# A planner that knows of the interface VectorE and GpSimd share: what a new instruction order does to a two-block kernel

## The chip, the cores and the metric

The kernel runs on one core of a Trainium2 chip. A core has engines that run their own instruction queues beside each other: TensorE (PE in the profile; PEld is its weight load), VectorE (DVE), ScalarE (ACT), GpSimd (POOL) and SyncE (SP, which issues the transfers here). The metric is the device time of one execution in microseconds, the median of several runs. Smaller is better.

## The reference

Two transformer-like blocks on 512 tokens of width 1024, all in float32:

```
first_block:  h = x + hybrid_mixer(rmsnorm(x))       # gMLP gating, a gated 31-tap convolution, an mLSTM
              h = h + cross_attention(rmsnorm(h), rmsnorm(mem))
              h = h + conv_glu(rmsnorm(h))           # width 2816
              x = rmsnorm(h)
second_block: x = layer_norm(a*x + nsa_pool_mixer(x))   # sparse attention and a pooling branch
              x = layer_norm(a*x + square(relu(x @ w1)) @ w2)    # width 4096
              x = layer_norm(a*x + gla_mixer(x))        # gated linear attention
              x = layer_norm(a*x + square(relu(x @ w1)) @ w2)
```

Nearly all of the arithmetic is in products with weights that come from HBM once.

## The kernel before

**Products in two parts.** Every float32 matrix is split into a high part, rounded to the type float32r that TensorE multiplies at its full rate, and a low part, the difference. A product is then three matmuls: high by high, high by low, low by high (`mm`). So every weight that arrives has to be split on the chip first. Weights come in units of 512 KB (`wunit`): a transfer into a raw tile `wr`, then for each half of 512 columns a cast into `wh` and a subtraction `wr - wh` into `wl`. The cast may be done by ScalarE or VectorE, the subtraction by VectorE or GpSimd. `xth`/`xtl`, `hid`, `o`, `yh`/`yl`, `v`, `ph`/`pl` are split activations, `ps` are the eight banks of PSUM in which products build up, `x` is the running state, `nat` a norm before it is transposed, `g` a norm's gain, `ident` the identity with which TensorE transposes. In the mixer `gs`, `mrun` and `mrs` hold the mLSTM's gates and their running sums (4 partitions of 512), `pw` weights made from them, and `gcv`, `tm` the sums and products of the 31-tap convolution: the products `tm` go to VectorE or ScalarE, all sums `gcv` to GpSimd.

**What sets the order.** No instruction order is written by hand. The code of the stages is run against a `Recorder`, which keeps every step with the engines that may do it. A `Plan` then plays the program with a price for each step (`price1`: microseconds on the engine) and a time after it until others see the result. At every turn each engine takes, of its ready steps that can start first, the one with the longest remaining way to the end; a step with two possible engines goes to the one on which it ends first. The plan is played again up to eight times with the latest starts of the last plan as ranks (`ROUNDS = 8`), and the shortest is kept. The kernel is then emitted in the order of the planned starts, each engine's queue in that order; only the order and the choice of engine come from the plan, the waits on the chip are semaphores. Room is planned too: 33 pages for weights and split blocks, 3 raw tiles, 8 banks. Where the plan leaves TensorE without work for over 1 us (`IDLE`) ahead of a bank's first product, `emit` fills the gap with products that nothing reads, one for each 0.216 us (`warm`: `ps<-ident`, 128x512), to keep the array's clock up. They are put into the program whether or not the gap is there on the chip.

The parts that the change touches, before it:

```
def split(...):            # of weights
    nc.add([[("scalar", "activation", (hi, src, AF.Copy), {})], [("vector", "tensor_copy", (hi, src), {})]],
           BIAS)
    self.either("tensor_sub", lo, src, hi.bitcast(F32), bias=BIAS)     # VectorE or GpSimd

def price1(eng, m, args, kw):    # for TensorE
    return max(n, 2 * width(args[1])) / 2400.0 + 0.0025

def run(self, prio=None):        # the choice of engine for a step with two forms
    if any(max(ready[i], free[x[0]]) + x[2] + x[4] < mine - 1e-9 for x in o.forms if x[0] != e):
        continue
```

`BIAS` (1.0 us) is added to VectorE's end when it is compared with the other engine's for a weight's cast or subtraction: VectorE gets the step only where it would end over 1 us earlier. The plan's own prices, which the change leaves, put a subtraction of 128x512 at half as much on VectorE as on GpSimd. In the trace all instructions carry line 487, the line of `emit` that issues them; in the changed kernel it is 509.

Of the kernel before, what the change touches and what calls it, by code (L numbers as in the profile page):

```python
# [14 lines left out]
PSUM = bass.MemoryType.PSUM  # L15
# [13 lines left out]
# room: pages of weights or of a split block, half pages, weights on their way in  # L29
# [5 lines left out]
BIAS = 1.0  # L35


class Op:
    """One step of the plan: instructions that one engine issues back to back."""
# [20 lines left out]
def run(ap):  # L60
    """Elements next to each other in a transfer."""
    n = 1
    for s, k in sorted((int(s), int(k)) for s, k in list(ap.ap)[1:]):
        if s != n:
            break
        n *= k
    return n


def region(ap):  # L70
    """The tile, the partitions and the set of elements (as bits) that an access touches."""
# [26 lines left out]
class Recorder:  # L98
    """Stands in for the engines: keeps what they are told to do for the plan."""
# [9 lines left out]
    def add(self, forms, bias=0.0):  # L109
        """forms: ways to do one step, each a list of calls to one engine; bias: time against VectorE's."""  # L110
# [17 lines left out]
        o.forms = [(f[0][0], f) + price(f) + (bias if f[0][0] == "vector" else 0.0,) for f in forms]  # L128
# [3 lines left out]
    @contextmanager  # L132
    def together(self):
        """Calls to one engine as one step."""
        self.held = []
        yield
        calls, self.held = self.held, None
        self.add([calls])
# [11 lines left out]
def price1(eng, m, args, kw):  # L150
# [5 lines left out]
    if eng == "tensor":  # L156
        if m == "transpose":
            return 0.109
        if "float32r" in str(args[1].dtype):
            return max(n, 2 * width(args[1])) / 2400.0 + 0.0025  # L160
        return 4 * max(n, 64) / 2400.0
# [25 lines left out]

def price(calls):
    """Time on the engine, and the time after it until others see the result."""
# [5 lines left out]
class Plan:  # L195
    """Orders the recorded steps: each engine takes the ready step with the longest way to the end."""
# [16 lines left out]
    def depend(self):  # L213
# [29 lines left out]
        # weights wait for an earlier unit's end, and nothing starts too far ahead of its use  # L243
# [17 lines left out]
        # late banks are taken when all that goes into them is there  # L261
# [30 lines left out]
    def rank(self):  # L292
        for o in reversed(self.ops):
            eng, _, d, lat, _ = o.forms[0]
# [12 lines left out]
    def run(self, prio=None):  # L307
        ops, N = self.ops, len(self.ops)
        P = prio or [o.prio for o in ops]
        free = dict.fromkeys(Recorder.ENGINES, 0.0)  # L310
        dma_issue = dma_data = 0.0
# [17 lines left out]
        def room(o):  # L329
            """Time from which the step's new tiles find room; None if they may not be taken yet."""  # L330
# [32 lines left out]
        for _ in range(N):  # L363
            best = None
            for e, q in queue.items():
# [4 lines left out]
                for i in q:  # L370
                    o = ops[i]
                    s = ready[i] if ready[i] > f else f
                    if mn is not None and s > mn:
                        continue
                    form = next(x for x in o.forms if x[0] == e)
                    if len(o.forms) > 1:
                        mine = s + form[2] + form[4]
                        if any(max(ready[i], free[x[0]]) + x[2] + x[4] < mine - 1e-9 for x in o.forms if x[0] != e):
                            continue
# [29 lines left out]
            _, calls, d, lat, _ = form  # L409
# [7 lines left out]
            else:  # L417
# [4 lines left out]
                end = free[e] = s + d  # L422
            o.start, o.end, o.pick, o.room = s, end, calls, taken
# [19 lines left out]
    def improve(self, n):  # L443
        """Plans again with the last plan's latest starts as ranks, and keeps the best plan."""
# [8 lines left out]
    def late(self):  # L453
        """Latest starts of the steps when each engine keeps its order, as priorities."""
# [16 lines left out]
    def emit(self, tc, warm):  # L471
        """warm: calls that keep the array's clock up, for a bank about to be used."""
# [17 lines left out]
class Split:  # L490
    """A float32 matrix as two float32r parts whose sum is exact."""
# [11 lines left out]
class Duo:  # L503
    """Two 128-row blocks of a split matrix, as one operand of the vector engines and as blocks."""
# [6 lines left out]
class Block:  # L511
# [19 lines left out]
    # ---- room  # L531
    def rules(self, quota, banks=(2, 10), pages=(2, 1000), halves=(0, 1000)):
        """For the steps from here on: units of weights at a time; of each kind of room, what a step ahead of
        its turn leaves free for those before it, and how many of them it may pass."""
# [3 lines left out]
    def ps(self, late=False):  # L538
        """A bank; late: not taken before all that goes into it is there."""
# [8 lines left out]
    def pair(self, s):  # L548
        """A split block of 512 columns in one page."""
# [19 lines left out]
    # ---- building blocks  # L569
    def warm(self, bank):  # L570
        """A product that nothing reads: TensorE runs at half its clock after some microseconds without work."""
# [10 lines left out]
    def turn(self, ps, srcs):  # L582
        """Transposes of 128-column pieces next to each other in a bank."""
# [4 lines left out]
    def either(self, method, *args, bias=0.0, **kw):  # L588
        """A step for VectorE or GpSimdE."""
# [19 lines left out]
    def wunit(self, loads, n=1024):  # L609
        """Streams one unit of weights in; loads: (view of the unit, DRAM source)."""  # L610
# [12 lines left out]
    def unit_t(self, w, c0):  # L623
        """128 columns of a [1024, n] weight."""
# [4 lines left out]
    def unit_n(self, w, r0):  # L629
        """128 rows of a [k, 1024] weight."""  # L630
        return self.wunit([(lambda r: r, w[r0:r0 + P, :])])

    def proj_t(self, u, xT):
        """One column block; the first ones of a stage go by halves of the tokens."""
# [8 lines left out]
    def rsqrt(self, v, mul, eps, v2=None):  # L643
        """(v * mul + eps) ** -0.5 by Newton's iteration from an integer seed; v2 adds to v."""
# [22 lines left out]
    # ---- norms between the stages  # L667
# [4 lines left out]
    def to_T(self, src, i):  # L672
        """Token tile i of natural activations into blocks."""
# [9 lines left out]
    def rms(self, x, g, n, fast=True):  # L683
        """n = norm of x."""
# [13 lines left out]
    def stats(self, x, n=512):  # L698
        """Mean and variance along the free axis, by pieces of n."""
# [17 lines left out]
    def rms_norm_x(self, g):  # L717
        """The norm in the place of x."""
# [45 lines left out]
    def tail(self, steps, norm, turn=True):  # L764
        """A stage's last projection and the norm after it, by token tiles."""
# [13 lines left out]
    def proj_n_steps(self, part, w, r0, alpha=None, us=None, fine=False):  # L779
        """x += part.T @ w[r0:], part: blocks; fine: smaller pieces for the last tokens."""  # L780
# [17 lines left out]
    def setup(self):  # L798
# [11 lines left out]
        # additive causal mask of a diagonal tile  # L810
# [7 lines left out]
    def pack(self, names):  # L818
        """Vectors of a multiple of 128 as columns, 128 to a column."""
# [19 lines left out]
    # ---------------------------------------------------------------- block 1  # L839
    def mix(self):  # L840
# [10 lines left out]
        # gates: the parts of their weights next to each other  # L851
# [44 lines left out]
        # xc, its convolution, and q, k, v  # L896
# [16 lines left out]
        def qkv(h):  # L913
# [10 lines left out]
            # two more columns of ones sum the rows of the scores  # L924
# [6 lines left out]
        # score rows of the key tiles: 0, 1 and 3 in a page, 2 in half of one  # L931
# [86 lines left out]
        # gated convolution  # L1018
# [11 lines left out]
        def taps():  # L1030
            """The convolution's taps: products on VectorE and ScalarE, sums on GpSimdE."""
# [38 lines left out]
        # spatial gating  # L1070
# [123 lines left out]
    def gate_proj(self, gu, xT):  # L1194
        """Both parts of narrow weights side by side in the columns, their products in the rows."""
# [10 lines left out]
    def mem(self):  # L1206
        """Keys and values of the memory."""
# [113 lines left out]
    # ---------------------------------------------------------------- block 2  # L1321
# [21 lines left out]
    def nsa(self, xT):  # L1343
# [5 lines left out]
        def stack(t, ps, g, scale=None):  # L1349
            """64 rows of group g as hi and lo halves of the 128 rows of t."""  # L1350
# [23 lines left out]
        def compress(s):  # L1374
            """Compressed keys (s = 0) or values of both groups."""
# [46 lines left out]
            else:  # L1422
                # rows: hi and lo parts of the scores, for each the blocks of both groups
# [8 lines left out]
        # keys with both halves of the rows alike: all hi, all lo  # L1432
# [12 lines left out]
        # queries: hi and lo halves of the rows, in heads b and 4 + b  # L1445
# [11 lines left out]
        # values and gates, token-major  # L1457
# [23 lines left out]
        # pooling branch  # L1481
# [32 lines left out]
        def cmp_attn(b, q):  # L1514
            """Attention of a pair of heads over the compressed blocks: gated scores, by blocks."""
# [360 lines left out]
```

## Time and profile before

| | |
|---|---|
| median of 3 runs | 2028.74 us (2028.26 to 2033.82) |
| profiled execution | span 2026.6 us from its first to its last instruction; the page gives no other time of it |
| PE | 1931.1 us busy, 95% |
| DVE | 1283.8 us busy, 63% |
| ACT | 804.4 us busy, 40% |
| POOL | 714.8 us busy, 35% |
| HBM | 177 MB moved, 88 GB/s |

Rows of groups read: line, engine, operation, out<-in with the buffers' numbers left out, sizes, how many, then busy time in us and mean ns of one, then idle time of that engine just before them and who ended it. Rows by stretch of time read: from:to, length, busy us (and instructions) of PE, PEld, DVE, ACT and POOL, the share of TensorE's clock that was granted, the share of time that DMA was busy, GB/s. In time: the first block's mixer runs to about 300 us, with the memory's keys and values from about 195; cross attention to about 450; the convolutional feed-forward to about 815; sparse attention to about 1050; the first MLP to about 1400; linear attention to about 1640; the second MLP and the last norm to the end.

### The profile page before, as it was taken

What the parts mean: (1) busy time and instruction counts of PE and PEld (TensorE: products, weight loads), DVE (VectorE), ACT (ScalarE), POOL (GpSimd) and SP (SyncE); (2) the same over time, 40 slices, a digit from 0 to 9 for tenths busy, and PEclk for the clock granted to TensorE, in tenths of its full rate; (3) what the DMA queues carried; (4) which work ended last, traced back from release to release, by engine and by line L of the source; (5) the groups of instructions that cost most, each with busy time, mean ns of one, the idle gap of its engine ahead of it and who ended that gap; (6) DMA issues with size and microseconds to landing.
All of it is one profiled execution on the core that took longest, in us unless ns stands there. A gap on an engine that the chain in (4) does not pass through costs nothing. (4 is left out here: it accounts for less than half of the span.)

```text
span 2026.6 us, 27236 instructions
## 1 busy us (share of the span) xinstructions
PE 1931.1 (95%) x10206; PEld 1632.6 (81%) x10206; DVE 1283.8 (63%) x2366; ACT 804.4 (40%) x1614; POOL 714.8 (35%) x571
## 2 busy tenths in 40 slices
PE   8978899999999999989999999999999999999998
PEld 7756778888888888878888777777999888778776
DVE  5899966564444456588984345467686774355457
ACT  4556435334322233576734223232465334122231
POOL 3767534213212333233644222233223234122232
PEclk9988999999999999999999999999999999999999
DMA  5212333223213333330332233332223322223231
GB/s 165 79 47 72 125 94 115 83 63 105 74 54 102 115 101 89 70 74 11 97 112 84 63 94 104 85 126 77 83 62 104 94 73 87 61 77 107 91 127 55
DMA packets 215470, 177.40 MB, mean 88 GB/s; under 512 B 25174, under 2 KB 194202, under 8 KB 215338
## 3 DMA queue, kind: packets, MB, share of 16 engines
q1 hardware_dynamic: 215338, 175.66, 29.6%
q8 instruction: 80, 1.31, 0.3%
q14 instruction: 52, 0.43, 0.1%
HBM read 173.54 MB, written 2.10 MB: 87 GB/s over the span
## 5 line engine op out<-in xcount | busy, mean ns | idle before, releaser
L487 POOL TENSOR_TENSOR wl<-wr,wh 128x512 fp32r<-128x512 f32 (+1 forms) x387 | 551.7, 1438 | 1093.3 <-PE ps L487 450.3
L487 PE MATMUL ps<-xth,wl 128*128 128x512 f32 (+1 forms) x1464 | 516.9, 353 | 4.9 <-DVE wl L487 4.3
L487 PE MATMUL ps<-xtl,wh 128*128 128x512 f32 (+1 forms) x1464 | 517.3, 353 | 3.8 <-DVE xtl L487 3.7
L487 PE MATMUL ps<-xth,wh 128*128 128x512 f32 (+1 forms) x1464 | 519.4, 355 | 0.1
L487 ACT ACTIVATE wh<-wr 128x512 fp32r<-128x512 f32 (+1 forms) x544 | 311.9, 622 | 462.9 <-PE ps L487 277.3
L487 PE MATMUL ps<-wh,hid 128*128 128x512 f32 (+1 forms) x1392 | 437.5, 392 | 1.4 <-ACT wh L487 1.3
L487 DVE TENSOR_TENSOR wl<-wr,wh 128x512 fp32r<-128x512 f32 x238 | 285.0, 1211 | 135.4 <-ACT wh L487 78.9
L487 PEld LDWEIGHTS ps<-xth,wl 128*128 128x128 f32 x1464 | 278.3, 190 | 47.0 <-DVE wl L487 5.8
L487 PEld LDWEIGHTS ps<-xtl,wh 128*128 128x128 f32 x1464 | 278.6, 190 | 44.6 <-DVE xtl L487 6.0
L487 PEld LDWEIGHTS ps<-xth,wh 128*128 128x128 f32 x1464 | 279.0, 191 | 40.1 <-ACT xth L487 0.5
L487 PEld LDWEIGHTS ps<-wh,hid 128*128 128x128 f32 x1392 | 261.1, 188 | 60.9 <-ACT wh L487 2.7
L487 PE MATMUL ps<-wl,hid 128*128 128x512 f32 (+1 forms) x696 | 275.0, 395 | 7.7 <-DVE wl L487 6.2
L487 DVE TENSOR_TENSOR x<-x,ps 128x512 f32<-128x512 f32 (+1 forms) x210 | 140.6, 677 | 155.7 <-PE ps L487 154.8
L487 PEld LDWEIGHTS ps<-wl,hid 128*128 128x128 f32 x696 | 131.2, 188 | 46.5 <-DVE wl L487 13.6
L487 DVE TENSOR_TENSOR r<-r 128x512 f32<-128x512 f32 x64 | 69.0, 1079 | 65.2 <-ACT r L487 64.7
L487 DVE CAST wh<-wr 128x512 fp32r<-128x512 f32 x81 | 45.8, 581 | 90.5 <-PE ps L487 83.7
L487 PE MATMUL ps<-wl,xth 128*128 128x256 f32 (+2 forms) x320 | 94.6, 296 | 1.3 <-DVE wl L487 1.0
L487 PE MATMUL ps<-wh,xth 128*128 128x256 f32 (+2 forms) x320 | 95.7, 299 | 0.0
L487 PE MATMUL ps<-wh,xtl 128*128 128x256 f32 (+2 forms) x320 | 94.3, 295 | 0.0
L487 POOL TENSOR_TENSOR gcv<-gcv,tm 128x511 f32<-128x511 f32 (+29 forms) x60 | 81.4, 1376 | 16.8 <-DVE tm L487 12.3
L487 DVE TENSOR_TENSOR hid<-r,hid 128x512 fp32r<-128x512 f32 x64 | 51.8, 810 | 43.0 <-ACT hid L487 42.4
L487 ACT ACTIVATE r<-ps 128x512 f32<-128x512 f32 x64 | 37.7, 589 | 90.6 <-PE ps L487 90.6
(355 smaller groups left out, 2718.2 us busy)
## 6 DMA issues: line engine op xcount, KB each, us to landing
wr<-in_mlp_w_dram SPq DMA_DIRECT2D x128, 512.0 KB
wr<-in_w_up_dram SPq DMA_DIRECT2D x44, 512.0 KB
wr<-in_c_w_in_dram SPq DMA_DIRECT2D x24, 512.0 KB
wr<-in_w_down_dram SPq DMA_DIRECT2D x22, 512.0 KB
wr<-in_w_in_dram SPq DMA_DIRECT2D x16, 512.0 KB
wr<-in_w_xkv_dram SPq DMA_DIRECT2D x16, 512.0 KB
wr<-in_w_out_dram SPq DMA_DIRECT2D x8, 512.0 KB
wr<-in_w_xq_dram SPq DMA_DIRECT2D x8, 512.0 KB
```

The costliest lines, as they stand in the source:

```text
L487: getattr(getattr(self.rec.nc, eng), method)(*args, **kw)
```

## The change

Three changes, all in the planner. (1) The interface to on-chip memory that VectorE and GpSimd share becomes a resource of the plan: `port` tells which steps need it (every GpSimd operation but fills and counters; of VectorE those with two inputs wider than one element in SBUF, and plain copies and `tensor_scalar` from SBUF to SBUF), and such a step starts only after the last one that held it. (2) `BIAS` becomes 0. (3) A matmul is priced by `n / 2285 + 0.007` us: 0.231 us in place of 0.216 for 512 columns, 0.119 in place of 0.109 for 256. Comments and docstrings are taken out besides, which does nothing.

```
-BIAS = 1.0
+BIAS = 0.0
...
-            return max(n, 2 * width(args[1])) / 2400.0 + 0.0025
+            return max(n / 2285.0 + 0.007, width(args[1]) / 1200.0 + 0.0025)
...
+def port(calls):
+
+    for eng, m, args, kw in calls:
+        if eng not in ("vector", "gpsimd") or m in ("memset", "iota", "dma_start"):
+            continue
+        out = kw["out"] if "out" in kw else args[0]
+        ins = [x for x in list(args[1:]) + [x for k, x in kw.items() if k not in ("out", "accum_out")] if is_ap(x)]
+        room = [x for x in ins if "PSUM" not in str(x.space) and width(x) > 1]
+        if eng == "gpsimd" or len(room) > 1:
+            return True
+        if m in ("tensor_copy", "tensor_scalar") and room and "PSUM" not in str(out.space):
+            return True
+    return False
...
+                    form = next(x for x in o.forms if x[0] == e)
+                    if form[5] and shared > s:
+                        s = shared
...
-                        if any(max(ready[i], free[x[0]]) + x[2] + x[4] < mine - 1e-9 for x in o.forms if x[0] != e):
+                        if any(max(ready[i], free[x[0]], shared if x[5] else 0.0) + x[2] + x[4] < mine - 1e-9
+                               for x in o.forms if x[0] != e):
...
                 end = free[e] = s + d
+                if locks:
+                    shared = end
```

The work of the program is the same; its order and the engines of some steps are not. Counted over the whole program: subtractions `wl` of 128x512 on VectorE 236 before and 537 now, on GpSimd 381 and 80; casts `wh` of 128x512 on ScalarE 536 and 406, on VectorE 81 and 211; ScalarE's table loads 45 and 40; products `ps<-ident` that nothing reads 38 and 131; SyncE's instructions 409 and 409.

TensorE's row in the mixer, around the transposes of the gates. Before, the transposes come between other products (`ps_102`, `ps_171`):

```order
L487 MATMUL ps_102_177<-wh_137_212,xth_15_90 128x512
L487 MATMUL ps_102_177<-wl_138_213,xth_15_90 128x512
L487 MATMUL ps_102_177<-wh_137_212,xtl_16_91 128x512
L487 MATMUL ps_84_159<-ident_74,gs_55_130 128x4 x4
L487 MATMUL ps_84_159<-ident_74,gs_56_131 128x4 x4
L487 MATMUL ps_112_187<-mrs_53_128,ident_74 128x512 x2
```

Now some 50 of the products that stood behind them stand ahead, and 34 products that nothing reads:

```order
L509 MATMUL ps_176_251<-xth_15_90,wl_175_250 128x512
L509 MATMUL ps_120_195<-qk_92_167,qk_94_169 128x256 x3
L509 MATMUL ps_84_159<-ident_74 128x512 x34
L509 MATMUL ps_84_159<-ident_74,gs_55_130 128x4 x4
L509 MATMUL ps_84_159<-ident_74,gs_56_131 128x4 x4
L509 MATMUL ps_112_187<-mrs_53_128,ident_74 128x512 x2
L509 MATMUL ps_182_257<-mrs_53_128,ident_74 128x512 x2
```

The gates' transposes are later in TensorE's row, with nothing useful right ahead of them. A second such place follows (21 products ahead of the first `ps<-v,ph`), and 9 and 13 stand ahead of two of the memory's products.

GpSimd's row in the mixer, where the memory's weights (`wl_416`, `wl_420`, `wl_425`) arrive beside the convolution's sums. Before:

```order
L487 TENSOR_TENSOR wl_416_491<-wr_414_489,wh_415_490 128x512 x2
L487 TENSOR_TENSOR wl_420_495<-wr_418_493,wh_419_494 128x512 x2
L487 TENSOR_TENSOR gcv_98_173<-gcv_98_173,tm_286_361 128x490
L487 TENSOR_TENSOR gcv_99_174<-gcv_99_174,tm_269_344 128x494
```

Now:

```order
L509 TENSOR_TENSOR gcv_99_174<-gcv_99_174,tm_269_344 128x494
L509 TENSOR_TENSOR gcv_99_174<-gcv_99_174,tm_271_346 128x493
L509 TENSOR_TENSOR gcv_98_173<-gcv_98_173,tm_286_361 128x490
L509 TENSOR_TENSOR cv_130_205<-cv_130_205,sig_242_317 128x512
L509 TENSOR_TENSOR gcv_98_173<-gcv_98_173,tm_316_391 128x489
L509 TENSOR_TENSOR wl_425_500<-wr_423_498,wh_424_499 128x512
```

The four subtractions of `wl_416` and `wl_420` have gone to VectorE, and one of the two of `wl_425`.

VectorE's row in the second MLP where pages come free for three units at once (`wl_2541`, `wl_2544`, `wl_2555`). Before, GpSimd does one half of each of these and VectorE the other:

```order
L487 SCALAR_TENSOR_TENSOR x_73<-x_73,ps_2506_2581 128x512
L487 CAST wh_2543_2618<-wr_2542_2617 128x512
L487 CAST wh_2554_2629<-wr_2553_2628 128x512
L487 TENSOR_TENSOR wl_2541_2616<-wr_2539_2614,wh_2540_2615 128x512
L487 TENSOR_TENSOR wl_2544_2619<-wr_2542_2617,wh_2543_2618 128x512
L487 TENSOR_TENSOR wl_2555_2630<-wr_2553_2628,wh_2554_2629 128x512
```

Now all six halves are VectorE's:

```order
L509 SCALAR_TENSOR_TENSOR x_73<-x_73,ps_2506_2581 128x512
L509 CAST wh_2543_2618<-wr_2542_2617 128x512
L509 TENSOR_TENSOR wl_2541_2616<-wr_2539_2614,wh_2540_2615 128x512
L509 CAST wh_2554_2629<-wr_2553_2628 128x512
L509 TENSOR_TENSOR wl_2544_2619<-wr_2542_2617,wh_2543_2618 128x512
L509 TENSOR_TENSOR wl_2555_2630<-wr_2553_2628,wh_2554_2629 128x512 x2
L509 TENSOR_TENSOR wl_2541_2616<-wr_2539_2614,wh_2540_2615 128x512
```

The first subtraction now stands behind one cast in place of two, and GpSimd does none of the six.

More of the change, by code (lines that the diff above doesn't have):

```diff
@@ L127, in add @@
             o.reads += [region(x) for x in ins if on_chip(x)]
-        o.forms = [(f[0][0], f) + price(f) + (bias if f[0][0] == "vector" else 0.0,) for f in forms]
+        o.forms = [(f[0][0], f) + price(f) + (bias if f[0][0] == "vector" else 0.0, port(f)) for f in forms]
         self.ops.append(o)
@@ L293, in rank @@
         for o in reversed(self.ops):
-            eng, _, d, lat, _ = o.forms[0]
+            d, lat = o.forms[0][2:4]
+            eng = o.forms[0][0]
             o.prio = max((self.ops[s].prio for s in o.succs), default=0.0) + d + lat
@@ L310, in run @@
         free = dict.fromkeys(Recorder.ENGINES, 0.0)
+        shared = 0.0
         dma_issue = dma_data = 0.0
@@ L372, in run @@
                     s = ready[i] if ready[i] > f else f
+                    form = next(x for x in o.forms if x[0] == e)
+                    if form[5] and shared > s:
+                        s = shared
                     if mn is not None and s > mn:
                         continue
-                    form = next(x for x in o.forms if x[0] == e)
                     if len(o.forms) > 1:
                         mine = s + form[2] + form[4]
-                        if any(max(ready[i], free[x[0]]) + x[2] + x[4] < mine - 1e-9 for x in o.forms if x[0] != e):
+                        if any(max(ready[i], free[x[0]], shared if x[5] else 0.0) + x[2] + x[4] < mine - 1e-9
+                               for x in o.forms if x[0] != e):
                             continue
@@ L408, in run @@
                     live[k].add(t)
-            _, calls, d, lat, _ = form
+            _, calls, d, lat, _, locks = form
             if e == "sync":
```

## The prediction

> **What bounds the kernel now.** The page first: TensorE.
>
> ```profile
> span 2026.6 us, 27236 instructions
> ...
> PE 1931.1 (95%) x10206; PEld 1632.6 (81%) x10206; DVE 1283.8 (63%) x2366; ACT 804.4 (40%) x1614; POOL 714.8 (35%) x571
> ```
>
> So TensorE sits idle for 2026.6 - 1931.1 = 95.5 us, and the change, which leaves its useful products alone, can win there or in the clock. The second view is busy time by stretch: length, then busy us (and count) of PE, PEld, DVE, ACT, POOL, the granted clock, the DMA share and rate.
>
> ```profile
> core 0: us, PE busy (x) PEld busy (x) DVE busy (x) ACT busy (x) POOL busy (x), PEclk, DMA share, GB/s
> 0.00:89.00 89.00, 75.96 (x449) 66.79 (x450) 59.39 (x110) 46.60 (x91) 41.05 (x43) 0.94 0.46 127
> 89.00:126.00 37.00, 29.14 (x135) 23.06 (x134) 36.08 (x71) 21.86 (x40) 27.14 (x22) 0.91 0.27 78
> 126.00:196.00 70.00, 55.39 (x272) 45.18 (x271) 67.78 (x186) 42.18 (x83) 48.29 (x50) 0.88 0.21 61
> 196.00:259.00 63.00, 54.45 (x327) 47.19 (x328) 60.97 (x178) 34.05 (x68) 34.88 (x26) 0.94 0.32 101
> ...
> 297.00:454.00 157.00, 149.49 (x899) 131.79 (x898) 97.51 (x198) 65.30 (x160) 51.34 (x37) 0.98 0.29 84
> 454.00:763.00 309.00, 308.57 (x1393) 252.57 (x1393) 142.86 (x176) 94.77 (x158) 87.33 (x61) 1.00 0.31 93
> 763.00:888.00 125.00, 116.44 (x711) 102.93 (x711) 83.23 (x176) 58.64 (x135) 40.05 (x37) 0.98 0.36 84
> 888.00:976.00 88.00, 85.01 (x560) 75.58 (x560) 76.68 (x217) 62.30 (x178) 28.45 (x39) 0.99 0.05 17
> 976.00:1330.00 354.00, 349.31 (x1687) 287.61 (x1687) 200.70 (x301) 125.19 (x240) 130.39 (x98) 1.00 0.32 92
> 1330.00:1396.00 66.00, 63.13 (x261) 49.29 (x260) 39.15 (x55) 15.01 (x27) 19.32 (x17) 0.97 0.37 122
> 1396.00:1626.00 230.00, 223.58 (x1585) 207.05 (x1584) 173.99 (x338) 114.55 (x214) 70.30 (x52) 1.00 0.29 83
> 1626.00:1816.00 190.00, 184.80 (x914) 154.10 (x913) 101.44 (x154) 58.77 (x110) 64.75 (x42) 0.98 0.27 78
> 1816.00:2027.00 211.00, 197.91 (x871) 159.33 (x869) 120.80 (x171) 53.68 (x94) 60.55 (x42) 0.98 0.29 93
> ```
>
> From 89 to 259 us, the mixer, VectorE is 97% busy (164.8 of 170) and TensorE idles 31.0 us; at a granted clock of 0.91, 0.88 and 0.94 another 3.3 + 8.4 + 3.8 = 15.5 us are lost. Elsewhere TensorE is the bound, VectorE about half busy, and idle time comes in pieces. So a third of what can be won lies where VectorE is the bound.
>
> Next, groups by shape: is VectorE's time its own?
>
> ```profile
> L487 DVE TENSOR_TENSOR wl<-wr,wh 128x512 fp32r<-128x512 f32 x236 | 283.0, 1213 | 135.4 <-ACT wh L487 78.9 <-PE ps L487 47.8 <-issue 7.6
> L487 DVE TENSOR_TENSOR x<-x,ps 128x512 f32<-128x512 f32 x206 | 139.0, 682 | 155.7 <-PE ps L487 154.8
> L487 DVE TENSOR_TENSOR r<-r 128x512 f32<-128x512 f32 x64 | 69.0, 1079 | 65.2 <-ACT r L487 64.7
> L487 DVE CAST wh<-wr 128x512 fp32r<-128x512 f32 x81 | 45.8, 581 | 90.5 <-PE ps L487 83.7 <-issue 3.7 <-DMA wr<-in_mlp_w_dram 2.9
> ```
>
> It is not. Three operations of one size: with one input in PSUM 682 ns, with both in SBUF 1079 and 1213. The excess over 682 alone is 236 x 0.531 + 64 x 0.397 = 151 us. GpSimd's side:
>
> ```profile
> L487 POOL TENSOR_TENSOR wl<-wr,wh 128x512 fp32r<-128x512 f32 x381 | 547.9, 1450 | 1087.0 <-PE ps L487 450.3 <-ACT wh L487 412.1 <-issue 118.0
> L487 POOL TENSOR_TENSOR gcv<-gcv,tm 128x511 f32<-128x511 f32 (+29 forms) x60 | 81.4, 1376 | 16.8 <-DVE tm L487 12.3
> ```
>
> The rule of the Trainium skill for this ("SBUF — State Buffer", Who interferes with whom) is that a VectorE instruction with two SBUF inputs and a GpSimd instruction that reads SBUF exclude each other for the whole instruction. The three rows agree with it. By it the excess could fall to nothing only where no GpSimd work is left.
>
> **The change, part by part.** *301 subtractions move from GpSimd to VectorE, 130 casts from ScalarE.* VectorE gains 301 x 0.68 = 205 us (a `wl` among the gate chain's rows below takes 0.67) and at most 130 x 0.58 = 75. GpSimd loses 301 x 1.450 = 436 us of 715; if the 151 us of waiting fall in proportion (they could stay, or go whole), 92 go. VectorE ends near 1284 + 205 + 75 - 92 = 1470 us, 74%: room everywhere but in the mixer. ScalarE loses about 81 us, which nobody waits for.
>
> *One place shows the price,* in the second MLP:
>
> ```profile
> 1750.00 1.86 DVE L487 CAST wh<-wr 128x512 fp32r<-128x512 f32 x2 [8.14 <-PE ps L487]
> 1751.79 4.04 DVE L487 TENSOR_TENSOR wl<-wr,wh 128x512 fp32r<-128x512 f32 x3
> ```
>
> ```profile
> 1750.28 4.40 POOL L487 TENSOR_TENSOR wl<-wr,wh 128x512 fp32r<-128x512 f32 x3 [29.84 <-PE ps L487]
> ```
>
> ```profile
> 1753.59 0.50 PE L487 MATMUL ps<-wl,hid 128*128 128x512 f32 x1 [1.77 <-DVE wl L487]
> ```
>
> Six subtractions and two casts take until 1755.8; TensorE waits 1.77 us for VectorE's first. With all on VectorE the first stands behind one cast and is done by 1750.0 + 0.58 + 0.68 = 1751.3, so that wait goes; all eight take about 2 x 0.58 + 6 x 0.68 = 5.2 us, no longer than now. For waits of this sort, outside the mixer, I take half of a stretch's idle time as won: none is one bound, all the other. What is late next there is ScalarE's half of the casts, or the transfer.
>
> *The gates' place (89 to 126).* VectorE's rows of the gate chain, then TensorE's:
>
> ```profile
> 79.94 0.67 DVE L487 SCALAR_TENSOR_TENSOR gs<-gs,gs 4x512 f32<-4x512 f32 x1
> ...
> 84.86 0.46 DVE L487 TENSOR_SCALAR tm<-yp,cols 128x507 f32<-128x507 f32 x1
> ...
> 88.40 0.67 DVE L487 TENSOR_TENSOR wl<-wr,wh 128x512 fp32r<-128x512 f32 x1
> 89.00 1.21 DVE L487 TENSOR_TENSOR_SCAN mrun<-gs 4x512 f32<-4x512 f32 x1
> ...
> 90.72 1.76 DVE L487 TENSOR_TENSOR gs<-gs,mrun 4x512 f32<-4x512 f32 x1
> ```
>
> ```profile
> 92.61 0.66 PE L487 MATMUL ps<-ident,gs 4*128 4x4 f32 x8
> ...
> 107.56 0.58 PE L487 MATMUL ps<-v,ph 128*128 128x258 f32 x1 [3.32 <-ACT ph L487]
> ```
>
> The chain runs for 12.6 us (79.94 to 92.5) beside useful products. In the new order its last part has only dead products beside it: 34, then 21 ahead of `ps<-v,ph`. At full clock one costs 25 / 110 = 0.227 us:
>
> ```profile
> 500.00:525.00 25.00, 25.00 (x110) 20.32 (x109) 14.30 (x16) 10.23 (x18) 6.50 (x5) 1.00 0.26 84
> ```
>
> So 55 x 0.227 = 12.5 us, in place of 7.9 idle and 3.3 of clock: -1 us, that is a loss. Bounds -6 (if the chain is late besides) and +5.
>
> *126 to 196.* Of GpSimd's 48.3 us these are subtractions:
>
> ```profile
> 126.00:196.00 70.00, 16.17 (x12) 0.88 0.21 61
> ```
>
> In the matching piece of the new order 3 of 12 are left, 14 of 17 sums, and 4 of 12 products `tm` on VectorE. What the two engines need one after the other falls by 9 x (1.35 - 0.68) + 3 x 1.36 + 8 x 0.46 = 13.8 us (16.17 / 12 = 1.35; 81.4 / 60 = 1.36; 0.46 by the row of `tm` above). The ceiling is idle and clock, 14.6 + 8.4 = 23. I take 14, bounds 0 and 23.
>
> *196 to 259.* GpSimd loses 14 of 15 subtractions, 14 x 1.35 = 19, VectorE gains 13 x 0.68 = 9, and 6 sums come later, 6 x 1.36 = 8: a net 2 to 5, and 22 dead products (5.0 us) fall in 8.6 us of idle time. I take 4, bounds -5 and 12.
>
> *The rest, half of the idle,* but for the start, where the first transfers set the time, and the last norm, which no product follows:
>
> ```profile
> 2000.00:2025.00 25.00, 16.90 (x97) 14.60 (x95) 22.76 (x55) 3.05 (x4) 7.08 (x6) 0.88 0.22 82
> ```
>
> That end holds 8.1 us and the 1.6 after it. 0 to 89 +2 of 13; 297 to 454 +3 of 7.5; 454 to 763 0; 763 to 976 +5 of 11.6; 976 to 1330 +2.5 of 4.7; 1330 to 1626 +4 of 9.3; 1626 to 1816 +3 of 5.2; 1816 on +2 of the 3.4 that the last norm leaves. Together +21.5.
>
> *Dead products elsewhere:* 93 more, 77 counted above; the other 16 x 0.227 = 3.6 us, hidden in the waits for `nat` and the sparse scores: I charge half, -2. *The price of a matmul* costs nothing by itself; 25 us hold 110 of 512 columns, so 0.231 fits the trace, and 0.216 let the plan think weights late. SyncE issues the same 409, some in another order; a raw tile is free as soon as its subtraction is done, sooner by the above.
>
> Sum: -1 + 14 + 4 + 21.5 - 2 = 36.5 us. Against the profiled span 2026.6 - 36.5 = 1990; the median is 2.1 above the span, so 1992 us.
>
> **The rivals.**
>
> *Nothing to measure.* TensorE is 95% busy and the idle time moves. If the mixer wins nothing and dead products stand where TensorE has work, 93 x 0.227 = 21.1 us eat the 21.5 won elsewhere: 2028. For it: they are executed whatever happens. Against: VectorE at 97% in the mixer leaves TensorE waiting somewhere.
>
> *Slower: VectorE's queue waits for weights.*
>
> ```profile
> ACT wh L487 <- DMA wr<-in_mlp_w_dram: 100.7, 37, 6.7
> ```
>
> ScalarE stands 100.7 us for transfers in the MLPs, up to 6.7 at once. With a third of the casts and most subtractions on VectorE the same waits stand in its row, ahead of `x<-x,ps`, `r` and `hid`, on which banks and the next products depend. If they reach TensorE in full: 2029 - 36 + 101 = 2093; it turns slower once about 42 of the 101 us reach it. Say 60%: 2053. Against: VectorE has 200.7 of 354 us busy there, and TensorE idles only 4.7 us now with ScalarE so held. The Trainium skill ("TensorE: Matmul & The Clock Gate", the part on the array) calls ScalarE's and VectorE's queues strict first-in first-out, which is what this rival needs; ScalarE's row above agrees.
>
> *The interface is nearly free.* With GpSimd at 40% of its work the mixer's waits could go almost whole: 31.0 + 15.5 us less 12.5 of dead products are 34, where I count 17: 1975. For it: what blocks VectorE there is mostly gone; against: the 60 sums `gcv` stay. The exclusion rule named above would bring the time there.
>
> **How the numbers follow.** Forecast 0.70, 1992 (its own range 1972 to 2015); free interface 0.12, 1975; nothing 0.11, 2028; slower 0.07, 2053. The range is 1965 to 2032, from the upper bounds of the mixer's terms to the case of nothing. About 0.3% is what a measurement here can tell from none: 2022.6 and 2034.8. Faster 0.82, same 0.11, slower 0.07.
>
> **What would show it.** POOL near 280 us, DVE near 1450; `wl` on VectorE below 0.9 us in the mean, `r<-r` below 0.85; 126 to 196 shorter by 10 us or more, its clock above 0.95; TensorE idle below 65 us. Wrong if the mean of `wl` stays above 1 us, if the mixer's end does not come earlier, if the 34 dead products are followed by a wait of the gates' transposes, or if `x<-x,ps` waits for its own row behind a transfer.

## The result and the profile after

The median went from 2029.67 us to 1976.53 us, a ratio of 0.9731 with a 95% interval of 0.9718 to 0.9745. The profiled executions take 2026.6 and 1975.0 us, so 51.6 us are to be found. First the changed kernel's page, its first two lines:

```profile
span 1975.0 us, 26969 instructions
...
PE 1924.9 (97%) x10299; PEld 1639.8 (83%) x10299; DVE 1280.3 (65%) x2791; ACT 744.8 (38%) x1501; POOL 258.7 (13%) x254
```

TensorE idles 50.1 us in place of 95.5. Not all of these 45.4 us are won: 93 more products that nothing reads, some 93 x 0.227 = 21 us, are counted as busy now. That the busy time falls by 6.2 us all the same means that the useful products take some 27 us less. VectorE runs 425 more instructions in 3.5 us less time. The groups by shape say how:

```profile
L509 DVE TENSOR_TENSOR wl<-wr,wh 128x512 fp32r<-128x512 f32 x537 | 374.4, 728 | 67.6 <-PE ps L509 50.0 <-ACT wh L509 12.7 <-issue 1.1
L509 DVE TENSOR_TENSOR x<-x,ps 128x512 f32<-128x512 f32 x206 | 139.3, 683 | 157.0 <-PE ps L509 156.6
L509 DVE TENSOR_TENSOR r<-r 128x512 f32<-128x512 f32 x64 | 44.2, 691 | 61.5 <-ACT r L509 61.2
L509 DVE CAST wh<-wr 128x512 fp32r<-128x512 f32 x211 | 88.7, 429 | 124.0 <-PE ps L509 73.7 <-DMA wr<-in_mlp_w_dram 35.1 <-DMA wr<-in_w_up_dram 7.3
```

The three operations of one size, which took 682, 1079 and 1213 ns, now take 683, 691 and 728. The one with an input in PSUM has not moved; the others have come down to it.

Then the stretches. Both traces are cut where TensorE has done the same amount of useful products: worth 62, 86, 130, 178 and 360 us at full clock (0.231 us for 512 columns, 0.119 for 256). As the order differs, they need not be the same products one by one. Of before:

```profile
0.00:89.20 89.20, 76.16 (x449) 66.95 (x450) 59.59 (x110) 46.80 (x91) 41.25 (x43) 0.94 0.46 127
89.20:126.10 36.90, 29.04 (x135) 22.95 (x134) 35.98 (x70) 21.66 (x40) 27.04 (x22) 0.91 0.27 78
126.10:196.20 70.10, 55.49 (x272) 45.32 (x271) 67.88 (x187) 42.38 (x84) 48.19 (x50) 0.88 0.21 61
196.20:258.80 62.60, 54.05 (x326) 46.83 (x326) 60.57 (x177) 33.65 (x68) 34.68 (x26) 0.95 0.32 102
258.80:453.80 195.00, 187.45 (x1059) 161.92 (x1059) 120.75 (x243) 76.98 (x183) 62.49 (x45) 0.98 0.32 92
453.80:2026.60 1572.80, 1528.95 (x7973) 1288.65 (x7971) 939.04 (x1585) 582.91 (x1152) 501.12 (x388) 0.99 0.29 86
```

And of the changed kernel:

```profile
0.00:77.50 77.50, 73.08 (x459) 64.85 (x460) 51.94 (x122) 40.58 (x82) 32.33 (x35) 1.00 0.51 139
77.50:129.30 51.80, 43.78 (x183) 35.09 (x182) 45.53 (x94) 38.26 (x68) 22.68 (x24) 0.87 0.26 75
129.30:184.30 55.00, 51.02 (x287) 43.06 (x287) 48.22 (x162) 37.65 (x75) 27.48 (x28) 0.97 0.17 49
184.30:244.70 60.40, 54.85 (x335) 48.49 (x335) 56.03 (x150) 33.84 (x68) 26.33 (x19) 0.97 0.41 128
244.70:432.50 187.80, 184.07 (x1064) 159.44 (x1063) 130.59 (x318) 71.37 (x172) 23.14 (x17) 1.00 0.31 94
432.50:1975.00 1542.50, 1518.09 (x7980) 1288.92 (x7978) 947.97 (x1949) 523.11 (x1040) 126.71 (x132) 1.00 0.30 87
```

The lengths, row by row, give 11.7, -14.9, 15.1, 2.2, 7.2 and 30.3 us won. I call the first five rows, up to the end of cross attention, the head (453.8 us, then 432.5) and the last the tail (1572.8, then 1542.5). Most was won in the tail, where TensorE is the bound.

What TensorE waits for, summed over the program, before and after (total, times, longest):

```profile
PE ps L487 <- DVE wl L487: 16.0, 17, 3.2
PE ps L487 <- DVE nat L487: 10.6, 8, 3.4
```

```profile
PE ps L509 <- DVE wl L509: 5.8, 12, 1.7
PE ps L509 <- DVE xtl L509: 3.6, 7, 1.1
...
PE ps L509 <- DVE gs L509: 3.2, 2, 2.9
PE ps L509 <- DVE nat L509: 2.9, 4, 1.2
```

### The profile page after: what moved, and what is told of

It reads as the page before. It is cut to its first block, busy times and chain, and to the rows that moved or that the text cites. A ratio compares the mean times of both kernels' runs of the same rounds, so it can differ in the third digit from the quotient of the medians.

```text
span 1975.0 us, 26969 instructions
## 1 busy us (share of the span) xinstructions
PE 1924.9 (97%) x10299; PEld 1639.8 (83%) x10299; DVE 1280.3 (65%) x2791; ACT 744.8 (38%) x1501; POOL 258.7 (13%) x254
## 4 chain that ended last, share of the span: by engine, by line
PE 79%; DVE 13%; DMA 2%; ACT 2%; issue 2%; SPq 1%; POOL 1%; DVEq 0%; ACTq 0%; POOLq 0%
PE ps L509 79%; DVE sm L509 3%; DVE wl L509 3%; SPq L509 1%; DMA wr<-in_w_up_dram 1%; DVE x L509 1%; DVE wh L509 1%; DMA wr<-in_mlp_w_dram 1%; DVE xtl L509 1%; DVE pt L509 0%; DMA wr<-in_a_w_out_dram 0%; DVE tm L509 0%; ACT wh L509 0%; DVE nat L509 0%; POOL gcv L509 0%
## 5 line engine op out<-in xcount | busy, mean ns | idle before, releaser
L509 ACT ACTIVATE wh<-wr 128x512 fp32r<-128x512 f32 x413 | 242.8, 624 | 510.3 <-PE ps L509 315.9
L509 DVE TENSOR_TENSOR wl<-wr,wh 128x512 fp32r<-128x512 f32 x542 | 377.2, 726 | 67.7 <-PE ps L509 50.0
L509 POOL TENSOR_TENSOR wl<-wr,wh 128x512 fp32r<-128x512 f32 (+1 forms) x83 | 112.2, 1361 | 1448.0 <-PE ps L509 940.3
L509 DVE CAST wh<-wr 128x512 fp32r<-128x512 f32 x212 | 88.8, 428 | 124.0 <-PE ps L509 73.7
L509 DVE TENSOR_TENSOR r<-r 128x512 f32<-128x512 f32 x64 | 44.2, 691 | 61.5 <-ACT r L509 61.2
L509 DVE SCALAR_TENSOR_TENSOR cv<-ps,cols,cv 128x511 f32<-128x511 f32 (+2 forms) x56 | 41.8, 746 | 40.3 <-ACT cv L509 39.6
```

The source lines that it names most:

```text
L509: getattr(getattr(self.rec.nc, eng), method)(*args, **kw)
```

## Experiments: the order or the engines

The change moves steps from engine to engine and puts them in another order. Theory 1 is that taking work off GpSimd wins, theory 2 that the new order does. Two kernels cross the two. In each, the plan is that of one kernel, and the engine of every step that two engines can do is written over with the other kernel's choice:

```
     plan.improve(ROUNDS)
+    for o, e in zip([o for o in plan.ops if len(o.forms) > 1], PICKS):   # PICKS: "sgsv...", from the other kernel
+        o.pick = next(f[1] for f in o.forms if f[0][0] == e)
```

Old order with new engines:

> The order of every step is that of the kernel before; only the engine of each step that two engines can do is taken from the changed kernel (364 steps leave GpSimd for VectorE, 186 leave ScalarE for VectorE). Theory 1, work off GpSimd: the time follows GpSimd's busy time, 715 us for 2029 and 259 us for 1976.5, so 0.115 us a us; GpSimd is near 260 us here, wl on VectorE near 0.75 us, and the time is 1977 to 1995. Theory 2, the order: VectorE's row is packed by a plan that had not foreseen this work, so the time stays at 2015 to 2045, though wl gets faster.

New order with old engines:

> The reverse: the changed kernel's order and its 131 dead products, with the engines of the kernel before. Theory 1: GpSimd is back near 715 us, wl on VectorE back near 1.2 us, r<-r near 1.05, the time 2015 to 2045. Theory 2: the order alone carries the gain, 1975 to 1995 whatever GpSimd does.

| median, us | engines of before | engines of the change |
|---|---|---|
| order of before | 2029 | 2009.2 (ratio 0.990, 0.988 to 0.992) |
| order of the change | 2044.3 (1.0075, 1.006 to 1.009) | 1976.5 (0.973, 0.972 to 0.9745) |

The first missed both expectations; in the second theory 1 had the time right, though `wl` came back to 1.02 us only and not to 1.2. The engines alone win 20 us. The order alone loses 15 us. With the engines it wins another 33. In the first kernel `wl` takes 733 ns on VectorE, as fast as in the changed kernel, so release from GpSimd does not explain those 33 us. Its tail (1564.5 us) has won only 8.3 of the 30.3 us, and its products still wait (total, times, longest):

```profile
PE ps L487 <- DVE wl L487: 13.6, 14, 4.0
PE ps L487 <- DVE nat L487: 7.1, 8, 1.4
```

Fast subtractions stand in a row that was planned without them. That is theory 3, formed here: the gain needs VectorE's prices on the chip to be those of the plan, and an order made from them. The plan prices a subtraction on VectorE at 0.068 + 512/960 = 0.601 us. In the changed kernel's second MLP, at the place that the prediction priced:

```profile
1704.92 0.43 DVE L509 CAST wh<-wr 128x512 fp32r<-128x512 f32 x1 [8.06 <-PE ps L509]
1705.27 0.68 DVE L509 TENSOR_TENSOR wl<-wr,wh 128x512 fp32r<-128x512 f32 x1
1705.87 0.42 DVE L509 CAST wh<-wr 128x512 fp32r<-128x512 f32 x1
1706.20 2.49 DVE L509 TENSOR_TENSOR wl<-wr,wh 128x512 fp32r<-128x512 f32 x4
```

Four take 2.49 us, that is one each (2.49 - 0.68) / 3 = 0.603 us and the last one's 0.68 to its end. Before, three took 4.04 us. The products with `wl` at this place no longer wait, where before TensorE waited 1.77 us.

## Experiments: one part at a time

The handicap taken away and nothing else (`BIAS = 0.0` in the kernel before):

> The kernel before with BIAS 0 and nothing else: 256 subtractions stay on GpSimd (390 before, 86 changed), 301 casts go to VectorE (86 before). Theory 1: GpSimd near 495 us, so 2029 - 0.115 x 220 = 2004, 1995 to 2013. Theory 2: without the interface in the plan nothing is won, 2022 to 2040.

2046.7 us, ratio 1.008 (1.0055 to 1.010): slower, and above both ranges. GpSimd's 552 us are fewer than before's 715, so theory 1's rule of 0.115 us a us falls. Its groups:

```profile
L510 DVE TENSOR_TENSOR wl<-wr,wh 128x512 fp32r<-128x512 f32 x372 | 308.1, 851 | 41.6 <-PE ps L510 24.6 <-ACT wh L510 10.7 <-issue 1.4
L510 POOL TENSOR_TENSOR wl<-wr,wh 128x512 fp32r<-128x512 f32 x245 | 363.8, 1498 | 1173.9 <-PE ps L510 511.8 <-ACT wh L510 243.6 <-issue 214.3
```

And the first line of TensorE's waits:

```profile
PE ps L510 <- DVE wl L510: 26.7, 22, 3.9
```

This plan fills VectorE as if it and GpSimd could run side by side. In the trace they hold each other up: a subtraction takes VectorE 0.851 us, where the plan has 0.601, and TensorE waits 26.7 us for VectorE's subtractions, where before it waited 16.0.

The interface and the new price, with the handicap back (`BIAS = 1.0` in the changed kernel):

> The changed kernel with BIAS at 1.0 again: the plan knows of the interface and has the new price of a matmul, but with the handicap it gives GpSimd 625 of the 641 weight subtractions (86 in the changed kernel). Theory 1: GpSimd near 1000 us, so 2029 + 0.115 x 290 = 2062, 2040 to 2080, slower than before. Theory 2, that it is the plan's knowledge of the interface that wins: 1975 to 2000.

2047.4 us, 1.009 (1.007 to 1.010): slower, as theory 1 said. The plan knows of the interface but answers it by giving GpSimd nearly all subtractions.

The new price of a matmul and nothing else (`n / 2285.0 + 0.007` in the kernel before):

> The kernel before with the new price of a matmul and nothing else; 387 subtractions on GpSimd (390 before), 36 dead products (38 before). Theory 3: GpSimd near 715 us and wl near 1.2 us, as before, so 2022 to 2036. Theory 4: 1995 to 2012.

2042.7 us, 1.006 (1.005 to 1.008): a little slower, against both expectations.

The interface and no handicap, with the old price:

> The changed kernel with the old price of a matmul (0.216 us for 512 columns): interface in the plan and BIAS 0 alone. 91 weight subtractions stay on GpSimd (86 changed), so GpSimd near 265 us. Theory 3, formed after the first four runs: the gain needs the engines and an order planned for them, and the price is a detail: 1972 to 1992. Theory 4: the price, by which the plan no longer thinks weights late, carries the 33 us that the order brings on top of the engines: 2000 to 2015.

1983.5 us, 0.977 (0.976 to 0.979), as theory 3 expected. Interface and handicap together bring 46 of the 53 us; the other three combinations that were run are slower than before. Two were not run: the interface alone, and no handicap with the new price.

## Experiments: the luck of the plan

The changed kernel with a price of a matmul 0.4% higher:

```
-            return max(n / 2285.0 + 0.007, width(args[1]) / 1200.0 + 0.0025)
+            return max(n / 2275.0 + 0.007, width(args[1]) / 1200.0 + 0.0025)
```

> The changed kernel with a matmul priced 0.4% higher (n / 2275 in place of n / 2285), which means nothing for the chip but makes the plan fall out another way: 95 subtractions on GpSimd (86), 162 dead products (131). Theory 3 in its strict form, the mechanism sets the time: 1972 to 1982. Theory 5, part of the gain is how this one plan happened to fall out: 1985 to 2005, with the dead products' 31 x 0.23 = 7 us as the smallest part of it.

2006.0 us, 0.987 (0.986 to 0.989): 29.5 us longer than the changed kernel, 1 us above theory 5's range and far outside theory 3's. Nearly all of it is one wait. Its line in the waits:

```profile
PE ps L509 <- DVE pw L509: 26.9, 1, 26.9
```

GpSimd's, VectorE's and TensorE's rows of the timeline at the place:

```profile
128.18 24.22 POOL L509 TENSOR_TENSOR gcv<-gcv,tm 128x493 f32<-128x493 f32 x22 [0.60 <-ACT tm L509]
...
152.35 0.54 POOL L509 TENSOR_SCALAR_AFFINE_SELECT pw<-pw 128x128 f32<-128x128 f32 x2
152.67 1.16 DVE L509 TENSOR_TENSOR pw<-ps,pw 128x512 f32<-128x512 f32 x2 [26.31 <-POOL pw L509]
...
153.42 4.63 PE L509 MATMUL ps<-ident 128*128 128x512 f32 x10 [26.86 <-DVE pw L509]
```

GpSimd sums 22 products of the convolution before it makes the mask of `pw`, which takes a quarter of a microsecond and on which VectorE and then TensorE wait. The tail of this kernel is 1548.0 us, 5.5 more than the changed kernel's. The next kernel ranks the masks first, with all else as in that one. Its plan is played anew, so other steps can move too: its dead products went from 162 to 114.

```
-        P = [p + drains.get(i, 0.0) for i, p in enumerate(P)]
+        P = [p + drains.get(i, 0.0) + (60.0 if ops[i].forms[0][1][0][1] == "affine_select" else 0.0) for i, p in enumerate(P)]
```

> The kernel with the price 0.4% higher (2006 us), where TensorE stands 27.2 us for pw at 126 to 153 us: the chain behind that wait is GpSimd's mask of pw (0.2 us), which stands behind some 22 sums gcv of 1.1 us in GpSimd's row. Here the plan ranks the masks 60 us more urgent, and nothing else is edited. If that row is the cause, the wait goes and the time is 1975 to 1988. If the higher price has harmed the plan as a whole, it stays at 1995 to 2010.

1980.7 us, 0.9755 (0.974 to 0.977): as expected if that row is the cause. That the wait itself is gone was not seen in a trace; the time alone speaks for it, and what the other moves did was not taken apart.

Head and tail, cut where the same amount of useful products is done, set luck apart from what repeats:

| kernel | head, us | tail, us |
|---|---|---|
| before | 453.8 | 1572.8 |
| changed | 432.5 | 1542.5 |
| old order, new engines | 443.4 | 1564.5 |
| new order, old engines | 460.6 | 1582.9 |
| interface and price, handicap back | 474.5 | 1569.8 |
| no handicap alone | 455.5 | 1588.5 |
| interface, no handicap, old price | 448.1 | 1533.2 |
| price alone | 470.5 | 1569.0 |
| price 0.4% higher | 460.2 | 1548.0 |

The three kernels with the interface in the plan and no handicap have tails of 1533 to 1548 us, and no other is under 1564. Their heads run from 432 to 460, on both sides of before's 454: part of the 21.3 us that the changed kernel won there is luck of the plan.

## Experiments: dead products, sharing, and what is left

The changed kernel without the 77 dead products between 60 and 250 us of the plan:

```
-            if o.room is not None and o.start - last > self.IDLE:
+            if o.room is not None and o.start - last > self.IDLE and not 60.0 < o.start < 250.0:
```

> The changed kernel without the products that nothing reads between 60 and 250 us of the plan (77 of the 131: 34, 21, 9, 13); order and engines the same. By the prediction's step the 34 and 21 cost 12.5 us and fill idle time there: if all of it is idle in any case, the time stays within 3 us (1974 to 1980), or gets up to 4 us longer where TensorE then runs at half clock behind a wait. If they hold useful products back, it falls by up to 77 x 0.23 = 17.7 us, to 1959.

1977.8 us, 0.974 (0.973 to 0.976): no difference from 0.9731. The gates' transposes in the timeline, here and in the changed kernel:

```profile
103.80 0.56 PE L509 MATMUL ps<-ident,gs 4*128 4x4 f32 x4 [8.05 <-DVE gs L509]
107.03 0.59 PE L509 MATMUL ps<-ident,gs 4*128 4x4 f32 x4 [2.67 <-DVE gs L509]
```

```profile
96.28 7.92 PE L509 MATMUL ps<-ident 128*128 128x512 f32 x34
104.46 0.41 PE L509 MATMUL ps<-ident,gs 4*128 4x4 f32 x4 [0.26 <-DVE gs L509]
107.77 0.41 PE L509 MATMUL ps<-ident,gs 4*128 4x4 f32 x4 [2.91 <-DVE gs L509]
```

Without the 34 dead products TensorE waits the 8 us that they took. The gates' chain on VectorE sets the time.

Is it sharing that costs, or waiting for GpSimd's results? One kernel puts the load back with hardly anybody waiting for it: 335 subtractions that nothing reads, 329 of them of 496 columns, for which ScalarE waits 5.8 us in all.

```
+    scratch = B.const.tile([P, 496], F32R, name="scratch")
...
+            o.pick = o.pick + [("gpsimd", "tensor_sub", (scratch[:, :n], hi[:, :n], hi[:, :n]), kw)]   # n up to 496
```

> The changed kernel, order and engines alike, and beside it 329 subtractions on GpSimd that nothing reads (the tile wh minus itself into a scratch tile, 496 columns), one behind each subtraction that went from GpSimd to VectorE. GpSimd is back at about 700 us, but nobody waits for it: what it costs is the sharing alone. If the shared interface is the cost: wl on VectorE near 1.2 us (0.728 in the changed kernel), VectorE near 1600 us, and with VectorE that full the time at 2020 to 2090. If it is the waits for GpSimd's results that cost: wl below 0.85 us and 1975 to 1990.

2080.1 us, 1.025 (1.023 to 1.026): 104 us slower than the changed kernel with the same order and engines. Its busy times, two groups, and the first line of TensorE's waits:

```profile
PE 1963.6 (94%) x10299; PEld 1656.4 (80%) x10299; DVE 1471.0 (71%) x2791; ACT 743.7 (36%) x1501; POOL 693.8 (33%) x589
```

```profile
L509 DVE TENSOR_TENSOR wl<-wr,wh 128x512 fp32r<-128x512 f32 x537 | 500.4, 962 | 57.8 <-PE ps L509 38.5 <-ACT wh L509 11.7 <-issue 3.9
...
L509 DVE TENSOR_TENSOR x<-x,ps 128x512 f32<-128x512 f32 x206 | 139.3, 682 | 144.8 <-PE ps L509 144.4
```

```profile
PE ps L509 <- DVE wl L509: 27.1, 37, 1.9
```

The time fell where the sharing theory put it; `wl` rose by less than expected, to 962 ns and not 1.2 us, and VectorE to 1471 us and not 1600. `x<-x,ps` is at 682 ns again. The rule of the Trainium skill ("SBUF — State Buffer", Who interferes with whom), that a VectorE instruction with two SBUF inputs contends with a GpSimd instruction that reads SBUF, and one with at most one SBUF input does not, unless it runs in a mode that uses two ports, agrees with both rows. Not every row followed: `r<-r` takes 695 ns here and 691 in the changed kernel. Not all of the 104 us need be sharing: GpSimd's own useful steps now stand behind the dead ones in its row. How much that costs was not measured.

The 86 subtractions that the changed kernel leaves on GpSimd, moved too, order held (`o.pick = o.forms[0][1]` for each):

> The changed kernel's order, and the 86 subtractions that it leaves on GpSimd (80 of them wl) taken by VectorE, each at the place that it had in time. GpSimd falls from 259 to about 148 us. Theory 1 (every microsecond of GpSimd's work costs): by the slope between the two kernels with the changed order, (2044 - 1976.5) / (707 - 259) = 0.15, the time falls by 17, to 1955 to 1968. Theory 3 (what matters is that plan and chip agree, and VectorE's row was planned without these 86): no gain, 1972 to 1985.

1982.0 us, 0.9766 (0.975 to 0.978): nothing won, as theory 3 expected. `wl` falls to 689 ns, the tail stays (1543.9 us), and the head gets 3.4 us longer.

Last, a version put together from these runs:

```
-        P = [p + drains.get(i, 0.0) for i, p in enumerate(P)]
+        P = [p + drains.get(i, 0.0) + (60.0 if ops[i].forms[0][1][0][1] == "affine_select" else 0.0) for i, p in enumerate(P)]
-                self.either("tensor_sub", lo, src, hi.bitcast(F32), bias=BIAS)
+                nc.vector.tensor_sub(lo, src, hi.bitcast(F32))
-    AHEAD = 60.0
+    AHEAD = 30.0
-    DRAIN = 20.0
+    DRAIN = 15.0
-    TABLE = 3.0
+    TABLE = 5.0
-            return max(n / 2285.0 + 0.007, width(args[1]) / 1200.0 + 0.0025)
+            return max(n / 2300.0 + 0.007, width(args[1]) / 1200.0 + 0.0025)
-            return 0.06 + n / 1920.0 + (0.065 * max(1, cols) if m == "tensor_scalar" else 0)
+            return 0.085 + n / 1920.0 + (0.065 * max(1, cols) if m == "tensor_scalar" else 0)
```

> A version put together from what the runs so far say: weight subtractions only on VectorE, masks of pw first, and a plan picked among many with slightly different constants (a matmul at n / 2300, a cast 0.025 us dearer, AHEAD 30, DRAIN 15, TABLE 5). Theory 3: GpSimd near 165 us, no single wait over 5 us in the mixer, and the waits behind cross attention no more than in the changed kernel, so 1945 to 1968. If the gain was used up at 80 subtractions, 1972 to 1985.

1961.3 us, 0.967 (0.965 to 0.968): faster than both kernels. Its busy times:

```profile
PE 1916.5 (98%) x10292; PEld 1633.8 (83%) x10292; DVE 1282.7 (65%) x2843; ACT 751.9 (38%) x1518; POOL 155.0 (8%) x185
```

Head 422.3, tail 1536.4. The plan was planned without those subtractions on GpSimd, where the kernel above only moved them. How much comes from that, from the masks, or from a well-falling plan was not taken apart.

## Why the prediction was right, and where it wasn't

The forecast of 1992 us had the sign and the range right, and stands 15 us above the result. By its own terms, against the spans:

| stretch of before | predicted, us | measured, us |
|---|---|---|
| 0 to 89 | +2 | +11.7 |
| 89 to 126, gates | -1 | -14.9 |
| 126 to 196 | +14 | +15.1 |
| 196 to 259 | +4 | +2.2 |
| 259 to 454 | +3 | +7.2 |
| 454 to the end, 16.5 of idle less 2 of dead products | +14.5 | +30.3 |
| sum | +36.5 | +51.6 |

**The mis-sized term is "the rest, half of the idle".** Its idle time came out a little better than said. In the tail it fell from 1572.8 - 1528.95 = 43.9 us to 1542.5 - 1518.09 = 24.4, by 19.5 where 14.5 were counted; between 259 and 454 it fell by 3.8 where 3 were. What the step left out is that TensorE's busy time for the same amount of useful products falls as well, by 10.9 us in the tail and 3.4 between 259 and 454. These 14.3 us and the 5.8 of idle are, but for rounding, the 20.0 by which the two rows miss; the rows ahead of them miss by 4.9 the other way.

About half of the 14.3 us can be the clock. These are the stretches behind 259 us in which the clock was granted at 0.50, before and after:

```profile
319.11:322.52 3.41, 3.03 (x16) 2.65 (x15) 2.72 (x5) 2.16 (x6) 2.38 (x2) 0.50 0.19 73
...
sum 31.51, PE 21.78 PEld 19.57 DVE 21.50 ACT 11.76 POOL 10.68; mean PE 3.63 PEld 3.26 DVE 3.58 ACT 1.96 POOL 1.78
```

```profile
835.81:839.22 3.41, 3.00 (x8) 2.48 (x9) 3.38 (x14) 3.37 (x7) 0.61 (x1) 0.50 0.39 94
986.00:989.41 3.41, 3.41 (x10) 2.67 (x9) 1.36 (x4) 0.63 (x1) 0.00 (x0) 0.50 1.01 245
...
sum 12.78, PE 6.41 PEld 5.14 DVE 7.56 ACT 4.00 POOL 0.61; mean PE 2.14 PEld 1.71 DVE 2.52 ACT 1.33 POOL 0.20
```

TensorE is busy in them for 21.78 us before and 6.41 after, and at half clock up to half of that is lost: 10.9 and 3.2, a difference of 7.7 us. Each of them but that of the last norm follows one or two waits of TensorE, of 2.91, 3.39, 2.92, 0.95 with 1.48, and 1.39 us before, of 1.34 and 1.71 after. So such a wait costs more than its own length, though not every one does: behind the 1.77 us in the second MLP the clock stayed. The prediction counted lost clock in the mixer alone, though the rows it showed had 0.97 to 0.99 in six later stretches: 157 x 0.02 + 125 x 0.02 + 88 x 0.01 + 66 x 0.03 + 190 x 0.02 + 211 x 0.02 = 16.5 us. What shortened the products by the rest, some 6.6 us, is not shown. Over the whole program the mean granted clock went from 0.982 to 0.992.

**The size of that idle term rested on a reason that carries only part of it.** The prediction argued with earlier subtractions. The crossed kernel has the fast ones in the old order, and its tail wins 8.3 us; the other 22.0 came only with an order planned for them.

**VectorE's total was wrong.** 1470 us were expected, 1280.3 came. The casts were too dear (one takes 0.429 us, not 0.58), and the waiting that was to fall "in proportion", by 92 of 151 us, fell further: on the two rows that made up the 151 by 236 x (1.213 - 0.728) + 64 x (1.079 - 0.691) = 139. The largest part lies where the prediction counted nothing. The rows of `wl`, `wh` and `r` together take 91.4 + 42.9 - 24.8 = 109.5 us more, yet VectorE's total falls by 3.5, so its other operations take 113 us less. Of these, 23 are products `tm` (40 before, 19 now, the others are ScalarE's); most of the rest are operations that are as many as before and got faster, as `hid<-r,hid` with 688 ns in place of 810.

**The gates' place** was the weakest step. It priced 55 dead products against idle time; they cost nothing either way, as the run without them shows. What costs is the chain, whose last `gs` ended at 92.5 us before and ends at 107.7 now. The first two stretches must be read together, since a wait for `xconv` moved from one to the other: -3.2 us where +1 was forecast; alone, the gates' -14.9 lies outside the bounds of -6 and +5. The sign that was to prove the forecast wrong, a wait of the gates' transposes behind the 34 products, did come (2.91 us) and was too small to matter by itself.

**The mixer's +14** came as +15.1, with VectorE at 48.2 of 55.0 us in place of 67.9 of 70.1. This is less of a hit than it looks: with the price 0.4% higher one wait in the mixer takes 26.9 us, and the kernel with the old price wins nothing in the products of this stretch (73.4 us for them, from 114.0 to 187.4, where before took 70.1).

**The rivals.** The case of nothing needed a mixer that wins nothing and dead products that cost; up to 259 us 14.1 us were won, and 77 dead products less changed nothing. The free interface gave the right time, 1975, for the wrong place: it needed the mixer's waits to go almost whole, and up to 259 us the gain is 14.1 of the 34 it counted. The slower rival's condition came true, its price didn't:

```profile
ACT wh L509 <- DMA wr<-in_mlp_w_dram: 118.4, 47, 7.8
DVE wh L509 <- DMA wr<-in_mlp_w_dram: 35.1, 24, 3.7
```

VectorE does stand before transfers, 35.1 us, and no wait of TensorE for `x`, `r` or `hid` is among the thirteen largest. The range held the result; its lower end of 1965 lies 4 us below what the upper bounds of the mixer's terms give, 1992 - 6 - 9 - 8 = 1969, for which the prediction gives no reason.

## What to carry to other kernels

When a planner sets the order, a price that is wrong because two engines share something harms twice: the engine is slower than planned, and everything around it is in the wrong place. So mend the model and let it choose the engines again together. Here the choice without the mended model was slower than before (no handicap alone, 2047 us), and so was the mended model with the old handicap (2047). And before a planned kernel's time is put down to a cause, change a constant by less than half a per cent: here that moved the time by 29.5 us, through one short step queued behind 22 long ones.

## What the runs showed of the hardware

Even a two-input operation on two elements a partition can wait until a GpSimd instruction ends. In the kernel with the price 0.4% higher:

```profile
114.11 1.85 POOL L509 TENSOR_TENSOR gcv<-gcv,tm 128x496 f32<-128x496 f32 x1 [1.64 <-DVE tm L509]
...
114.77 1.21 DVE L509 SCALAR_TENSOR_TENSOR sm<-sm,sm 128x2 f32<-128x2 f32 x1
```

VectorE's 1.21 us end at 115.98, GpSimd's at 115.96; such an operation otherwise takes 0.14 to 0.16. The planner's `port` lets the one-element ones through as if they needed nothing, but `sm<-sm,sm` of 128x1 follows GpSimd's load too: 283 ns in the mean before, 224 in the changed kernel, 204 with the last subtractions moved:

```profile
L509 DVE SCALAR_TENSOR_TENSOR sm<-sm,sm 128x1 f32<-128x1 f32 x213 | 46.1, 224 | 3.8
```

A cast with one input is held up as well: 581 ns before, 429 in the changed kernel, 491 with GpSimd's load put back.
